# The shift and scale products of an adaLN front: eight weight units asked for at once, multiplied unsplit in four parts of the array

## The chip, the cores and the metric

The kernel runs on one core of one Trainium2 chip. The metric is device time in microseconds (us) of one execution. Before the change it was 1428.91 us, the median of three runs (1427.53 to 1434.31).

## The reference

One layer of a diffusion trunk over 256 latent and 256 context tokens of width 1024. What the change touches is the first step, the modulation vectors, and the projection that needs two of them:

```python
silu_c = jax.nn.silu(c)
silu_cc = jax.nn.silu(c_ctx)
sh1_l, sc1_l, g1_l, sh2_l, sc2_l, g2_l = jnp.split((silu_c @ w_ada[l] + b_ada[l])[:, None, :], 6, axis=-1)
sh1_c, sc1_c, ... = jnp.split((silu_cc @ w_ada[l] + b_ada[l])[None, None, :], 6, axis=-1)
pl = (xl * (1.0 + sc1_l) + sh1_l) @ w_in[l]
pc = (xc * (1.0 + sc1_c) + sh1_c) @ w_in[l]
yc, yl = token_mixers(pc, pl, ...)        # Hyena, short convolution, GLA, gated DeltaNet
xl = layer_norm(DN_ALPHA * xl + g1_l * (yl @ w_out[l]), ...)
fl = moe_ffn(xl * (1.0 + sc2_l) + sh2_l, ...)   # top 4 of 32 experts, all 32 are streamed
```

`w_ada` is 1024 x 6144 in fp32. Sections 0 and 1 of its columns (shift and scale, 8 MB) are needed for both vectors, `c` and `c_ctx`, before any projection can start. The other four sections are needed for `c` alone and much later.

## The kernel before

The program has two halves. The front (0 to about 375 us) makes the modulation vectors, the projections and the four token mixers. The expert stage (the rest) streams 384 units of 1 MB of expert weights through a ring of 16 places. The front's work is written as six generators that `weave` advances by a fixed string `ORDER`; what each engine executes, and in which order, is settled when the program is built. All loads go out on one queue, SP's, in program order; SP stops at a load whose place is not free yet.

A weight unit is 128 partitions x 2 rows x 1024 columns (1 MB) and lies in one of four places r0 to r3. `first_ada` names the eight units of sections 0 and 1, `('ada', sec, h)`, and `queues` deals them to the four places, two to a place. `issue(spot)` loads the next unit of a place and whatever `beside` ties to it; `done(key)`, called where a unit has been used for the last time, issues the next one of that place. So the second unit of a place is asked for after the product of the first, and the unit that follows (`uB`, the weights of the first projection B, or `uada` of section 2, the first of the late sections) after the product of the second.

`ada_first` multiplies the units. Of the two k rows of a unit one (`kk` = 0) is split: ACT copies it rounded to fp32r (`hi`, line 434), DVE subtracts to get `lo` (line 435), and TensorE multiplies both with the 4 columns of `s4` (line 438). The other row is multiplied as plain fp32 with the 2 columns of `sT3` (line 429). Both go to rows 0 to 3 of two PSUM banks. `ada_tail` copies these 4 rows out (lines 449 and 451), turns them with eight transposes (line 455) and adds bias and halves (lines 458 to 461). The result is `mod`.

Then `prep` modulates the inputs `xu` chunk by chunk (`modulate`, lines 543 to 545: ACT makes hi, DVE lo), splits the weights (`split`, lines 552 and 553: `hlB`), and `proj_toks` multiplies (lines 557 to 559, `pB`), 12 products of 432 columns for each of 8 chunks k. In between, ACT and POOL work on the late sections: `ada_late` scales a unit on ACT (line 643) and adds it up on POOL (lines 645, 647); its place is then loaded again. These steps stand in ACT's order between chunks of B: the first unit of section 2 after the third chunk.

Of the kernel before, what the change touches and what calls it, by code (L numbers as in the profile page):

```python
# [11 lines left out]
F32 = mybir.dt.float32  # L12
# [11 lines left out]
D = 1024  # L24
# [174 lines left out]
def trunk(ctx: ExitStack, tc: tile.TileContext, I, out, offs, dbg=None, nexp=NE):  # L199
# [65 lines left out]
    def load(dst, src):  # L265
        nc.sync.dma_start(dst, src)
# [17 lines left out]
    load(va[:, 0:64], I['va'][:, 0:64])  # L284

# [23 lines left out]
    beside['ada', 1, 3] = [(xus[0], xT[0])]  # L309
    beside['B', 0] = [(xus[1], xT[1])]  # L310
# [4 lines left out]
    first_ada = [('ada', sec, h) for sec in range(2) for h in range(4)]  # L315
# [7 lines left out]
    def issue(spot):  # L323
# [21 lines left out]
        for dst, src in beside.pop(key, []):  # L345
            load(dst, src)
        open_units[key], spot_of[key] = u, spot

    def take(key):
        return open_units[key]  # L350

    def done(key):

        issue(spot_of[key])

    for spot in range(4):
        issue(spot)

# [47 lines left out]
    sT = cst.tile([128, 16], F32, name="sT")  # L406
# [3 lines left out]
    s4 = cst.tile([128, 8, 4], F32R, name="s4")  # L410
    sT3 = sT.rearrange("p (k v) -> p k v", v=2)
    S_.activation(s4[:, :, 0:2], sT3, AF.Copy)
    V.tensor_sub(s4[:, :, 2:4], sT3, s4[:, :, 0:2])


    def ada_first():

        tails = []
        for sec in range(2):
            ps = [(bank, fbank)[sec](f"psada{sec}{n}") for n in range(2)]  # L420
            for h in range(4):
                if sec == 1:
                    next(tails[0], None)
                u = take(('ada', sec, h))
                for kk in range(2):
                    k = 2 * h + kk
                    if kk:
                        for n in range(2):
                            P_.matmul(ps[n][0:2], sT3[:, k], u[:, kk, n * 512:(n + 1) * 512], start=False, stop=(k == 7), skip_group_check=True)  # L429
                        done(('ada', sec, h))  # L430
                    else:
                        w2 = early([128, 2, D], F32R, (0, 1, 3)[(4 * sec + h) % 3], f"adap{sec}{k}")
                        hi, lo = w2[:, 0], w2[:, 1]
                        S_.activation(hi, u[:, kk], AF.Copy)
                        V.tensor_sub(lo, u[:, kk], hi)
                        for w in (hi, lo):
                            for n in range(2):
                                P_.matmul(ps[n][0:4], s4[:, k], w[:, n * 512:(n + 1) * 512], start=(k == 0 and w is hi), stop=False, skip_group_check=True)  # L438
                    yield
            tails.append(ada_tail(sec, ps))  # L440
        yield from tails.pop()
        have.add('mod')

    def ada_tail(sec, ps):

        r4 = fp.tile([128, D], F32, tag="kTn", name=f"r4{sec}")[0:4]
        for n in range(2):
            if sec and n:
                V.tensor_copy(r4[:, n * 512:(n + 1) * 512], ps[n][0:4])
            else:  # L450
                S_.activation(r4[:, n * 512:(n + 1) * 512], ps[n][0:4], AF.Copy)
        yield
        pt = xbank(f"psadT{sec}")
        for c in range(8):
            P_.transpose(pt[:, 4 * c:4 * c + 4], r4[:, c * 128:(c + 1) * 128], ident[0:4, 0:4])
        yield
        p4 = pt[:, 0:32].rearrange("p (c v) -> p c v", v=4)
        V.tensor_tensor(mod[:, sec], p4[:, :, 0:2], bada[:, 8 * sec:8 * sec + 8].unsqueeze(2).to_broadcast([128, 8, 2]), op=OP.add)
        V.tensor_tensor(mod[:, sec], mod[:, sec], p4[:, :, 2:4], op=OP.add)
# [241 lines left out]
    mst = early(list(I["masks"].shape), I32, 3, "mst")  # L701
    load(mst, I['masks'])
# [1407 lines left out]
```

## Time and profile before

| | us |
|---|---|
| median of 3 runs | 1428.91 |
| lowest, highest | 1427.53, 1434.31 |
| the profiled execution | 1435.11 |
| its span in the profile | 1433.3 |
| TensorE busy (81% of the span) | 1156.2 |
| ACT busy | 298.1 |
| DVE busy | 485.9 |

The profile is one execution; its span is the time from the first to the last recorded instruction, 1.8 us short of that execution's own time. TensorE's busy share is an average over two halves that have little in common, so it is not a limit by itself. What matters for the change stands in the first 60 us, of which the page's 40 slices (36 us each) show only two digits; these have to be read from the timeline and from narrower stretches. The moved bytes of a stretch are its GB/s times its length.

### The profile page before, as it was taken

The page shows a single profiled execution, that of the slowest core. Times are in us where ns is not written, and L with a number is a line of the kernel's source. Part 1 is how long each engine was busy: PE and PEld are TensorE (multiplying, and loading weights), DVE is VectorE, ACT ScalarE, POOL GpSimd, SP SyncE. Part 2 cuts the span into 40 slices and gives each one's busy share as a digit, 9 for nine tenths or more (in the row PEclk, how much of TensorE's full clock was granted, in tenths as well). Part 3 has the DMA queues.
Part 4 walks back from the last instruction along what each step waited for, and adds up shares of the span by engine and source line. Part 5 has one row for each costly group of instructions (what it writes and reads, how often), then busy time and mean ns, then how long its engine had stood idle before and what let it go on. Part 6 is the DMA issues. An engine that isn't in the chain of part 4 may idle for free.

```text
span 1433.3 us, 26137 instructions
## 1 busy us (share of the span) xinstructions
PE 1156.2 (81%) x11226; PEld 713.9 (50%) x11226; DVE 485.9 (34%) x857; ACT 298.1 (21%) x576; POOL 191.0 (13%) x233
## 2 busy tenths in 40 slices
PE   5797999889687897878698988777676979777883
PEld 0576888678544544445344633344333544444442
DVE  3767667978521211211020221121121111211116
ACT  2556644444210110101010111010001101001112
POOL 0242233440200100001000100000000100000002
PEclk9998879999698998989699999897869989877896
DMA  7733334427796998999965999999999999999960
GB/s 275 254 110 123 119 119 149 149 95 293 307 418 264 410 419 352 419 416 418 378 235 192 417 419 418 417 416 419 418 413 418 406 411 420 399 418 419 417 264 29
DMA packets 129056, 460.56 MB, mean 321 GB/s; under 512 B 9488, under 2 KB 19088, under 8 KB 128048
## 3 DMA queue, kind: packets, MB, share of 16 engines
q1 hardware_dynamic: 128816, 457.52, 80.4%
q8 instruction: 131, 2.15, 0.6%
q14 instruction: 109, 0.89, 0.2%
HBM read 456.45 MB, written 1.05 MB: 319 GB/s over the span
## 4 chain that ended last, share of the span: by engine, by line
PE 53%; DMA 24%; DVE 11%; issue 8%; ACT 4%; SPq 0%; DVEq 0%; ACTq 0%
PE g L1768 17%; DMA ring<-in_w_down 12%; PE four L1768 12%; DMA ring<-in_w_up 8%; PE xb L1750 6%; PE four L1814 2%; DMA ring<-in_w_gate 2%; PE fb L1786 2%; PE psada L429 1%; DMA bd<-in_b_down 1%; DMA uada<-in_w_ada 1%; PE psW L1005 1%; DVE gt L1794 1%; ACT scr L1796 1%; PE psada L438 1%
## 5 line engine op out<-in xcount | busy, mean ns | idle before, releaser
L1768 PE MATMUL g<-ring,X 128*32 128x256 f32 (+1 forms) x3680 | 350.1, 466 | 141.7 <-issue 89.0
L1768 PEld LDWEIGHTS g<-ring,X 128*32 128x32 f32 (+1 forms) x3680 | 153.8, 127 | 319.6 <-issue 228.6
L1768 PE MATMUL four<-ring,X 128*32 128x256 f32 (+1 forms) x2272 | 211.1, 440 | 20.0 <-DMA ring<-in_w_down 19.0
L1824 DVE SCALAR_TENSOR_TENSOR rows<-four,cw,rows 128x1024 f32<-128x1024 f32 x62 | 76.7, 1279 | 339.9 <-PE four L1814 339.9
L1794 DVE TENSOR_TENSOR gt<-fb,vc 128x256 f32<-128x256 f32 (+1 forms) x37 | 18.6, 504 | 405.1 <-PE fb L1786 405.1
L1750 PEld LDWEIGHTS xb<-Sg,hl 128*128 128x128 f32 x1024 | 133.8, 211 | 29.2 <-issue 26.5
L1768 PEld LDWEIGHTS four<-ring,X 128*32 128x32 f32 (+1 forms) x2272 | 86.3, 119 | 123.7 <-issue 61.5
L1750 PE MATMUL xb<-Sg,hl 128*128 128x96 f32 x1024 | 143.9, 300 | 4.7 <-DVE Sg L1736 2.6
L1736 POOL TENSOR_SCALAR Sq<-slots,rank 128x128 f32<-128x128 f32 x62 | 39.5, 648 | 563.4 <-PE xb L1758 333.5
L1772 ACT ACTIVATE sA<-g 128x256 f32<-128x256 f32 (+1 forms) x33 | 14.0, 423 | 331.3 <-PE g L1768 331.3
L1736 POOL TENSOR_SCALAR Sg<-slots,rank 128x96 f32<-128x96 f32 x62 | 31.7, 523 | 307.3 <-PE xb L1750 271.0
L645 POOL TENSOR_TENSOR adas<-adas,uada 128x1024 f32<-128x1024 f32 x24 | 59.1, 2464 | 100.7 <-ACT uada L643 100.3
L1752 ACT ACTIVATE X<-xb 128x384 f32<-128x384 f32 x64 | 31.4, 491 | 132.6 <-PE xb L1750 127.1
L1796 ACT ACTIVATE scr<-gt 128x256 f32<-128x256 f32 (+1 forms) x37 | 17.7, 480 | 158.7 <-DVE gt L1795 158.7
L1814 PE MATMUL four<-sA,ST 32*128 32x256 f32 (+1 forms) x512 | 46.5, 440 | 1.8 <-DVE sA L1988 1.8
L1772 ACT ACTIVATE sA<-four 128x256 f32<-128x256 f32 (+1 forms) x30 | 12.8, 427 | 167.3 <-PE four L1768 167.3
L643 ACT ACTIVATE uada<-uada,sT 128x1024 f32<-128x1024 f32 x32 | 35.7, 1142 | 9.8 <-DMA uada<-in_w_ada 9.8
L1005 PEld LDWEIGHTS <-before 64*64 64x64 f16 x1088 | 29.9, 116 | 9.8 <-issue 4.0
L1814 PEld LDWEIGHTS four<-sA,ST 32*128 32x128 f32 (+1 forms) x512 | 30.1, 206 | 7.6 <-DVE sA L1988 2.3
L1802 DVE TENSOR_TENSOR X<-fb,vc 128x256 f32<-128x256 f32 (+1 forms) x36 | 18.0, 499 | 41.3 <-PE fb L1786 41.3
L1797 DVE TENSOR_TENSOR gt<-gt,scr 128x256 f32<-128x256 f32 (+1 forms) x37 | 18.9, 510 | 21.9 <-ACT scr L1796 21.9
L1786 PE MATMUL fb<-cons,sB 128*128 128x128 f32 x76 | 15.5, 300 | 7.4 <-ACT sB L1772 7.4
(565 smaller groups left out, 1558.7 us busy)
## 6 DMA issues: line engine op xcount, KB each, us to landing
ring<-in_w_gate SPq DMA_DIRECT2D x128, 1024.0 KB, 18.0
ring<-in_w_up SPq DMA_DIRECT2D x128, 1024.0 KB, 17.8
ring<-in_w_down SPq DMA_DIRECT2D x128, 1024.0 KB, 18.3
uada<-in_w_ada SPq DMA_DIRECT2D x24, 1024.0 KB, 5.4
uout<-in_w_out SPq DMA_DIRECT2D x4, 1024.0 KB, 4.8
uE<-in_w_in SPq DMA_DIRECT2D x2, 1024.0 KB, 5.5
uF<-in_w_in SPq DMA_DIRECT2D x4, 512.0 KB, 4.0
uG<-in_w_in SPq DMA_DIRECT2D x2, 1024.0 KB, 5.2
```

Source lines behind the costliest of these rows:

```text
L643: S_.activation(u[:, kk], u[:, kk], AF.Copy, scale=sT3[:, 2 * h + kk, 0:1])
L645: G_.tensor_tensor(acc_, acc_, u[:, kk], op=OP.add)
L1005: P_.matmul(ps[cs, x * 64:x * 64 + 64], L[cs, x], R[cs, x] if len(R.shape) == 3 else R[cs], start=True, stop=True, skip_group_check=True)
L1736: eng.tensor_scalar(Sm[:, t, 0:m * n].rearrange("p (q s) -> p q s", s=n), slots[:, a:a + n].unsqueeze(1).to_broadcast([128, m, n]), rank[: ...
L1750: P_.matmul(xb[:, o:o + n], hl[:, t, k * 128:(k + 1) * 128], Sm[:, t, 0:n], start=(k == ks[0] and t == 0), stop=(t == 1), skip_group_check ...
L1752: S_.activation(X[:, ks[0] * n:(ks[-1] + 1) * n], xb[:, 0:len(ks) * n], AF.Copy)
L1768: P_.matmul(ps[n * q:n * q + n, 0:m], x(k), w[:, kk * 1024 + q * m:kk * 1024 + (q + 1) * m], start=(k == 0), stop=(k == 7), skip_group_che ...
L1786: P_.transpose(fb[:, c * 128:(c + 1) * 128], s[:, c * 128:(c + 1) * 128], ident)
L1794: V.tensor_tensor(g, p, bias(Cv('bg'), e, n), op=OP.add)
L1796: S_.activation(sg, g, AF.Sigmoid, scale=1.702)
L1814: P_.matmul(four[:, b, t * 256:(t + 1) * 256], st_[n * q:n * q + n, t * 128:(t + 1) * 128], Y[n * q:n * q + n, i * 256:(i + 1) * 256], sta ...
L1824: V.scalar_tensor_tensor(a, ps[t], cw[:, t, e:e + 1], a, op0=OP.mult, op1=OP.add)
```

## The change

All eight units of sections 0 and 1 are asked for at the start. The four of section 1 get places of their own for this: three ring places that are used later (r4, r5, r7) and a half of the buffer `pa`. The input `xT` (two loads) and the masks follow at once, the masks in the buffer `pb` instead of a ring place. `queues` then holds, behind the first unit of each place, what stood behind the second.

The product is no longer split. `s32` is a stationary operand of 32 columns, of which 2 are used and 30 are zero. The four products of a unit (2 rows x 2 halves of 512 columns) go to four 32-row parts of one PSUM bank, and so to four 32-column parts of the array, as plain fp32. Where a unit took 6 products before (4 of hi and lo, one record each in the profile, and 2 plain ones, two records each), it now takes 4 plain ones: 8 records before and after, of 512 columns each. The tail copies the whole bank (128 x 512) on ACT, turns it with four 128 x 128 transposes and adds the two parts that belong together, and the bias, on DVE.

The tile `s4` (128 bytes a partition) goes and `sT` grows by 128, so that what is allocated behind them starts where it did: all ring places stay 256 bytes above a multiple of 512. Which of the eight ring places lies where is permuted, since a place is laid out when it is first named.

```diff
+    extra = [early([128, 2048], F32, i, f"uada1{i}") for i in (0, 1, 3)] + [pa[:, 2048:4096]]
...
-    beside['ada', 1, 3] = [(xus[0], xT[0])]
-    beside['B', 0] = [(xus[1], xT[1])]
...
-    first_ada = [('ada', sec, h) for sec in range(2) for h in range(4)]
+    first_ada = [('ada', 0, h) for h in range(4)]
...
+        if key[0:2] == ('ada', 0):
+            h = key[2]
+            open_units['ada', 1, h], spot_of['ada', 1, h] = extra[h].rearrange("p (k f) -> p k f", k=2), None
...
     for spot in range(4):
         issue(spot)
+    for h in range(4):
+        load(take(('ada', 1, h)), w_ada[:, 2 * h:2 * h + 2, D:2 * D])
+    mst = pb[:, 2048:2048 + I["masks"].shape[1]].bitcast(I32)
+    for dst, src in ((xus[0], xT[0]), (xus[1], xT[1]), (mst, I['masks'])):
+        load(dst, src)
...
-    sT = cst.tile([128, 16], F32, name="sT")
+    sT = cst.tile([128, 48], F32, name="sT")[:, 0:16]
...
-    s4 = cst.tile([128, 8, 4], F32R, name="s4")
-    S_.activation(s4[:, :, 0:2], sT3, AF.Copy)
-    V.tensor_sub(s4[:, :, 2:4], sT3, s4[:, :, 0:2])
+    s32 = pb[:, 3200:3456].rearrange("p (k v) -> p k v", v=32)
+    V.memset(s32, 0.0)
+    V.tensor_copy(s32[:, :, 0:2], sT3)
...
-                    k = 2 * h + kk
-                    if kk:
-                        for n in range(2):
-                            P_.matmul(ps[n][0:2], sT3[:, k], u[:, kk, n * 512:(n + 1) * 512], start=False, stop=(k == 7), skip_group_check=True)
-                        done(('ada', sec, h))
-                    else:
-                        w2 = early([128, 2, D], F32R, (0, 1, 3)[(4 * sec + h) % 3], f"adap{sec}{k}")
-                        hi, lo = w2[:, 0], w2[:, 1]
-                        S_.activation(hi, u[:, kk], AF.Copy)
-                        V.tensor_sub(lo, u[:, kk], hi)
-                        for w in (hi, lo):
-                            for n in range(2):
-                                P_.matmul(ps[n][0:4], s4[:, k], w[:, n * 512:(n + 1) * 512], start=(k == 0 and w is hi), stop=False, skip_group_check=True)
-                    yield
+                    for n in range(2):
+                        q = 2 * kk + n
+                        P_.matmul(ps[32 * q:32 * q + 32], s32[:, 2 * h + kk], u[:, kk, n * 512:(n + 1) * 512], start=(h == 0), stop=(h == 3), skip_group_check=True)
+                done(('ada', sec, h))
+                yield
...
-        r4 = fp.tile([128, D], F32, tag="kTn", name=f"r4{sec}")[0:4]
...
+        r = t512(f"r{sec}")
+        S_.activation(r, ps, AF.Copy)
...
-        for c in range(8):
-            P_.transpose(pt[:, 4 * c:4 * c + 4], r4[:, c * 128:(c + 1) * 128], ident[0:4, 0:4])
+        for c in range(4):
+            P_.transpose(pt[:, 128 * c:128 * c + 128], r[:, c * 128:(c + 1) * 128], ident)
```

SP's order, before, from the last load of the first batch (`mst`, the masks) to the first projection's second unit. `uada_1_h` is unit h of section 1, `xu0` and `before0` the two halves of the input, `uB_0` and `uB_1` the units of B; in brackets the semaphores that a load waits for, of which DMAHW0 to DMAHW7 count the completion of earlier loads:

```order
L266 DMA mst_119<-in_masks 128x1152
L266 DMA uada_1_0_150<-in_w_ada 128x2x1024 [waits DMAHW0_49,DMAHW1_49,DVE_49,PE_49]
L266 DMA uada_1_1_185<-in_w_ada 128x2x1024 [waits DMAHW3_49,DVE_49,PE_49]
L266 DMA uada_1_2_196<-in_w_ada 128x2x1024 [waits DMAHW2_49,DMAHW4_49,DVE_49,PE_49]
L266 DMA uada_1_3_207<-in_w_ada 128x2x1024 [waits DMAHW5_49,DVE_49,PE_49]
L266 DMA xu0_92<-in_xT 128x2048
L266 DMA uB_0_224<-in_w_in 128x4x384 [waits DMAHW0_49,DVE_49,PE_49]
L266 DMA uB_0_224<-in_w_in 128x4x32 [waits DMAHW6_49]
L266 DMA uB_0_224<-in_w_in 128x4x16 [waits DMAHW7_49]
L266 DMA before0_84<-in_xT 128x2048
```

The same stretch now, from the first unit of section 1 (`uada10`; `uada11`, `uada13` and `before0<-in_w_ada` are the other three):

```order
L266 DMA uada10_87<-in_w_ada 128x2x1024
L266 DMA uada11_88<-in_w_ada 128x2x1024 [waits DMAHW0_49]
L266 DMA uada13_89<-in_w_ada 128x2x1024 [waits DMAHW1_49]
L266 DMA before0_84<-in_w_ada 128x2x1024 [waits DMAHW2_49]
L266 DMA xu0_95<-in_xT 128x2048 [waits DMAHW3_49]
L266 DMA before0_84<-in_xT 128x2048 [waits DMAHW4_49]
L266 DMA before1_85<-in_masks 128x1152 [waits DMAHW5_49]
L266 DMA uB_0_151<-in_w_in 128x4x384 [waits DMAHW6_49,PE_49]
L266 DMA uB_0_151<-in_w_in 128x4x32 [waits DMAHW7_49]
L266 DMA uB_0_151<-in_w_in 128x4x16 [waits DMAHW0_49]
```

The four units of section 1, the input and the masks no longer wait for PE or DVE, only each for the load that stands eight before it. The loads behind them (`uB_1`, `vb`, `cons`, then `uada_2_0`, the first unit of section 2) stand in the same order in both programs.

TensorE's order, before, from the last split row to the first product of B (`psada` are the products of section 1, `psadT1` its transposes, `pB0` the first bank of B):

```order
L438 MATMUL psada10_210<-adap16_274,s4_110 4x512 [waits Activation_49]
L438 MATMUL psada11_211<-adap16_274,s4_110 4x512
L438 MATMUL psada10_210<-adap16_274,s4_110 4x512 [waits DVE_49]
L438 MATMUL psada11_211<-adap16_274,s4_110 4x512
L429 MATMUL psada10_210<-uada_1_3_207,sT_106 2x512 [waits DMAHW3_49]
L429 MATMUL psada11_211<-uada_1_3_207,sT_106 2x512
L455 MATMUL psadT1_286<-cons2_89,r41_283 128x4 [waits Activation_49]
L455 MATMUL psadT1_286<-cons2_89,r41_283 128x4 x3
L455 MATMUL psadT1_286<-cons2_89,r41_283 128x4 [waits DVE_49]
L455 MATMUL psadT1_286<-cons2_89,r41_283 128x4 x3
L557 MATMUL pB0_298<-hlB0_308,xl0_115 128x432 [waits Activation_49]
```

The same place now, from the last but one unit:

```order
L438 MATMUL psada1_199<-uada13_89,before1_85 32x512 [waits DMAHW1_49]
L438 MATMUL psada1_199<-uada13_89,before1_85 32x512 x3
L438 MATMUL psada1_199<-before0_84,before1_85 32x512 [waits DMAHW2_49]
L438 MATMUL psada1_199<-before0_84,before1_85 32x512 x3
L452 MATMUL psadT1_235<-cons2_92,r1_233 128x128 [waits DVE_49,Activation_49]
L452 MATMUL psadT1_235<-cons2_92,r1_233 128x128 x3
L556 MATMUL pB0_243<-hlB0_253,xl0_124 128x432 [waits Activation_49]
```

A unit's product now waits for the unit's load alone; before, it waited for ACT and DVE too. Behind the first product of B the orders of all engines are the same as before.

## Rows read from the trace of the kernel before

**Rows 1.** The chain of waits from 44 to 56 us (start, us, what).

```profile
43.80 1.82 PE psada L429 x4
45.64 8.20 DMA uada<-in_w_ada
```

**Rows 2.** The timeline of SP (start, us, what it issues).

```profile
4.82 0.46 SPq L266 DMA_DIRECT2D mst<-in_masks  x1
15.02 16.63 SPq L266 DMA_DIRECT2D uada<-in_w_ada  x4
...
45.64 13.37 SPq L266 DMA_DIRECT2D uada<-in_w_ada  x2
```

**Rows 3.** Stretches of the first 54 us: busy times, granted clock, DMA share, GB/s.

```profile
core 0: us, PE busy (x) PEld busy (x) DVE busy (x) ACT busy (x) POOL busy (x), PEclk, DMA share, GB/s
0.00:53.80 53.80, 36.06 (x99) 9.74 (x100) 24.17 (x48) 16.71 (x25) 1.40 (x5) 0.90 0.81 293
0.00:6.00 6.00, 0.00 (x0) 0.00 (x0) 0.36 (x2) 1.72 (x3) 0.19 (x4) 1.00 0.64 192
6.00:16.00 10.00, 7.59 (x14) 1.11 (x14) 4.58 (x8) 2.53 (x3) 0.00 (x0) 1.00 1.02 418
20.00:26.00 6.00, 5.32 (x9) 0.85 (x10) 2.54 (x3) 2.31 (x3) 0.00 (x0) 0.51 0.00 0
28.00:36.00 8.00, 5.73 (x17) 0.95 (x16) 2.36 (x2) 4.09 (x5) 0.00 (x0) 1.00 1.01 357
36.00:52.00 16.00, 12.70 (x49) 4.61 (x48) 9.72 (x24) 6.07 (x11) 0.00 (x0) 0.93 1.00 356
52.00:54.00 2.00, 2.00 (x9) 1.89 (x8) 1.93 (x6) 0.14 (x1) 0.00 (x0) 0.70 0.16 66
```

**Rows 4.** The timeline of ACT around the first chunks of B.

```profile
47.45 0.60 ACT L543 ACTIVATE xl<-xu,mod 128x256 fp32r<-128x256 f32 x1 [2.07 <-DMA vb<-in_vb]
...
51.33 0.55 ACT L552 ACTIVATE hlB<-uB 128x432 fp32r<-128x432 f32 x1
53.86 2.19 ACT L643 ACTIVATE uada<-uada,sT 128x1024 f32<-128x1024 f32 x2 [1.99 <-DMA uada<-in_w_ada]
...
64.28 2.18 ACT L643 ACTIVATE uada<-uada,sT 128x1024 f32<-128x1024 f32 x2
```

**Rows 5.** Groups by line and shape, 0 to 48 us (busy us, mean ns | idle before).

```profile
L429 PE MATMUL psada<-uada,sT 128*2 128x512 f32 x32 | 18.4, 705 | 0.0
L438 PE MATMUL psada<-adap,s 128*4 128x512 f32 x32 | 10.4, 442 | 10.7 <-ACT adap L434 9.8 <-DVE adap L435 0.9
L434 ACT ACTIVATE adap<-uada 128x1024 fp32r<-128x1024 f32 x8 | 8.2, 1049 | 8.8 <-DMA uada<-in_w_ada 8.8
L451 ACT ACTIVATE r<-psada 4x512 f32<-4x512 f32 x3 | 1.8, 587 | 15.0 <-PE psada L429 15.0
```

**Rows 6.** The timeline, single rows of TensorE and DVE.

```profile
21.72 3.57 PE L429 MATMUL psada<-uada,sT 128*2 128x512 f32 x4
...
49.05 0.46 PE L557 MATMUL pB<-hlB,xl 128*128 128x432 f32 x1 [2.26 <-ACT hlB L552]
...
56.58 2.17 DVE L544 TENSOR_SCALAR xu<-xu,mod 128x256 f32<-128x256 f32 x1 [2.14 <-ACT xl L543]
...
395.53 1.07 PE L1768 MATMUL g<-ring,X 128*32 128x256 f32 x16
```

**Rows 7.** Transposes of 128 x 128, by line (ns min/median/max).

```profile
L1011 PE MATMUL pstk<-cons,kvT x8: 270/272/276, 111.2 to 112.7; 128*128 128x128 f32 x8
```

**Rows 8.** TensorE alone in stretches of B (busy, granted clock, DMA share, GB/s).

```profile
50.00:53.00 3.00, 2.68 (x7) 0.50 0.67 268
53.00:70.00 17.00, 13.51 (x66) 0.99 0.54 187
70.00:77.00 7.00, 5.92 (x16) 0.52 0.78 257
```

**Rows 9.** One stretch of the expert stage, columns as in rows 3.

```profile
1000.00:1100.00 100.00, 79.53 (x612) 39.37 (x602) 16.21 (x27) 9.51 (x21) 6.43 (x12) 0.83 1.03 417
```

More of the change, by code (lines that the diff above doesn't have):

```diff
@@ L352, in done @@
     def done(key):
-        issue(spot_of[key])
+        if spot_of[key] is not None:
+            issue(spot_of[key])
     for spot in range(4):
         issue(spot)
+    for h in range(4):
[3 more added lines that the diff above has]
+        load(dst, src)
     places = {}
@@ L419, in ada_first @@
         for sec in range(2):
-            ps = [(bank, fbank)[sec](f"psada{sec}{n}") for n in range(2)]
+            ps = (bank, fbank)[sec](f"psada{sec}")
             for h in range(4):
@@ L424, in ada_first @@
                 u = take(('ada', sec, h))
+                yield
                 for kk in range(2):
-                    k = 2 * h + kk
-                    if kk:
-                        for n in range(2):
-                            P_.matmul(ps[n][0:2], sT3[:, k], u[:, kk, n * 512:(n + 1) * 512], start=False, stop=(k == 7), skip_group_check=True)
-                        done(('ada', sec, h))
-                    else:
-                        w2 = early([128, 2, D], F32R, (0, 1, 3)[(4 * sec + h) % 3], f"adap{sec}{k}")
-                        hi, lo = w2[:, 0], w2[:, 1]
-                        S_.activation(hi, u[:, kk], AF.Copy)
-                        V.tensor_sub(lo, u[:, kk], hi)
-                        for w in (hi, lo):
-                            for n in range(2):
-                                P_.matmul(ps[n][0:4], s4[:, k], w[:, n * 512:(n + 1) * 512], start=(k == 0 and w is hi), stop=False, skip_group_check=True)
-                    yield
+                    for n in range(2):
+                        q = 2 * kk + n
+                        P_.matmul(ps[32 * q:32 * q + 32], s32[:, 2 * h + kk], u[:, kk, n * 512:(n + 1) * 512], start=(h == 0), stop=(h == 3), skip_group_check=True)
+                done(('ada', sec, h))
+                yield
             tails.append(ada_tail(sec, ps))
@@ L444, in ada_tail @@
     def ada_tail(sec, ps):
-        r4 = fp.tile([128, D], F32, tag="kTn", name=f"r4{sec}")[0:4]
[L447 to L451, printed above, removed]
+        r = t512(f"r{sec}")
+        S_.activation(r, ps, AF.Copy)
         yield
         pt = xbank(f"psadT{sec}")
-        for c in range(8):
-            P_.transpose(pt[:, 4 * c:4 * c + 4], r4[:, c * 128:(c + 1) * 128], ident[0:4, 0:4])
+        for c in range(4):
+            P_.transpose(pt[:, 128 * c:128 * c + 128], r[:, c * 128:(c + 1) * 128], ident)
         yield
-        p4 = pt[:, 0:32].rearrange("p (c v) -> p c v", v=4)
-        V.tensor_tensor(mod[:, sec], p4[:, :, 0:2], bada[:, 8 * sec:8 * sec + 8].unsqueeze(2).to_broadcast([128, 8, 2]), op=OP.add)
-        V.tensor_tensor(mod[:, sec], mod[:, sec], p4[:, :, 2:4], op=OP.add)
+        p4 = pt.rearrange("p (c k n v) -> p k n c v", c=4, k=2, n=2)[:, :, :, :, 0:2]
+        m = mod[:, sec].rearrange("p (n c) v -> p n c v", n=2)
+        b = bada[:, 8 * sec:8 * sec + 8].rearrange("p (n c) -> p n c", n=2).unsqueeze(3).to_broadcast([128, 2, 4, 2])
+        V.tensor_tensor(m, p4[:, 0], b, op=OP.add)
+        V.tensor_tensor(m, m, p4[:, 1], op=OP.add)
         if sec == 1:
@@ L698, in rsqrt2 @@
         V.scalar_tensor_tensor(dst, u, 3.0, less, op0=OP.subtract, op1=OP.mult)
-    mst = early(list(I["masks"].shape), I32, 3, "mst")
-    load(mst, I['masks'])
     G_.tensor_copy(masks, mst)
```

## The prediction

> **What bounds the kernel now.** I read the stretches first, then SP's timeline, then the chain and ACT's timeline around 50 us. Through the first 54 us everything goes over one stream of loads, and that stream stops. It moves 418 GB/s from 6 to 16 us and nothing from 20 to 26 [rows 3], because SP put nothing more into the queue: the first batch was out at 4.82 + 0.46 us, the next unit was asked for at 15.02, and the four units of section 1 took until 31.7 to be asked for, each after a product on TensorE [rows 2]. The page's DMA digits for the first slice (7 tenths) hide this hole.
>
> The chain between 44 and 56 us shows what the delay costs: the last product of the shift and scale ends at 45.62, and what follows is the load of the first unit of section 2, 8.20 us [rows 1]. ACT stands still for it 1.99 us, until 53.86, with the fourth chunk of B queued behind it [rows 4]; DVE waits 2.14 us for that chunk in turn and then works on B without a pause [rows 6]. So the place to watch is not the moment at which `mod` is ready, 47.45 at the latest [rows 4], but the landing of that unit. What comes later (the mixers, then the expert stage, which streams at 417 GB/s, a DMA share of 1.03 [rows 9]) keeps its order and is moved as a whole. Where it starts earlier, it ends earlier.
>
> **The loads.** Until that unit has landed, both programs load the same bytes: 293 GB/s over 53.8 us [rows 3] are 15.76 MB. In both it is the last of them. Its last bytes come at about 52.4 us (66 GB/s for the last 2 us are 0.13 MB, 0.4 us at 356 GB/s [rows 3]), and ACT starts 1.5 us behind that.
>
> Now no load before B waits for TensorE. The order shows that a load waits for the one eight places ahead of it; with seven or eight asked for, mostly of 1 MB, the stream does not run dry. So the first 16 us stay as they are: 192 x 6 + 418 x 10 give 5.33 MB [rows 3], and 10.43 MB remain. From there the rate decides, and the trace has two. With a batch of eight out it was 418; from 28 to 36 and from 36 to 52, with few loads out and B's small ones among them, 357 and 356, at a DMA share of 1.00 all the same [rows 3].
> - All at 418: 10.43 / 0.418 = 25.0, the unit lands at 16 + 25.0 + 1.5 = 42.5.
> - All at 356: 29.3, it lands at 46.8.
> - By kind: up to the masks 6.60 MB at 418 (15.8 us, to 31.8), then B's two units, vb, cons and the unit itself, 3.83 MB by their shapes, at 356 (10.8 us): 42.6 + 1.5 = 44.1.
>
> I take 44.6, the middle of the two ends, which lies next to the value by kind. Against 53.86 ACT's step is 9.2 us earlier; the ends give 7.1 and 11.4.
>
> The Trainium skill has a rule that speaks for the low end ("DMA: Bandwidth & Descriptors", section "Where 436 GB/s comes from"): the fabric could carry about 435 GB/s, but from HBM a core gets about 358. The trace does not bear it out as a limit, since 418 and 417 stand in rows 3 and 9. By it the unit would land at 46.6 and the gain would be 7.2, inside the ends above.
>
> **The products.** ACT loses eight copies of 1049 ns (8.2 us), DVE their eight differences, TensorE 18.4 + 10.4 us of products [rows 5]. None of that is a term of the sum, since the loads now set the pace. What is added on TensorE is 8 records of 512 columns for each unit, in four parts. Nearest row: in the expert stage 16 records of 256 columns, four parts as well, the same number of columns, take 1.07 us [rows 6]. That is at full clock; at half it is 2.1, still less than the 2.5 us in which 1.05 MB come at 418. The other end is no overlap at all: four plain records of 512 columns took 3.57 us at half clock [rows 6], so 7.1 a unit. I take 1.07 to 2.1, the row with the four parts.
>
> The last unit of section 1 is the ninth MB: 9.24 MB by 16 + 3.91 / 0.418 = 25.4, landed at 26.9. Behind it: product 1.1 to 2.1, the copy on ACT (587 ns for the same 512 columns [rows 5]; 128 partitions instead of 4, taken as the same), four transposes of at most 272 ns each, twice that at half clock [rows 7], three small DVE steps, and hand-overs of some 0.2 us: 3 to 6 us. `mod` is ready between 30 and 33. B's first unit lands at 31.8 + 0.885 / 0.356 + 1.5 = 35.8. So the products and the longer tail are hidden by 3 to 6 us; from there on each us more would move the first chunk, and from some 7 us on the fourth as well, because ACT needs only 4.4 us for three chunks (47.45 to 51.88 [rows 4]).
>
> B's first product moves from 49.05 [rows 6] to about 36.4, 12.6 us. Of that lead 3.4 us are given back at once: ACT is through with three chunks at about 39.3 and then waits some 5.3 us for the unit of section 2 instead of 1.99. What is late next is therefore the same load as before, and the gain is that of the load, 9.2. The next unit is asked for when POOL has used the first, moves with it, and was in time before (ACT took it at 64.28 without a wait [rows 4]).
>
> **Rest.** The masks are turned by POOL some 16 us later; POOL has nothing else until the unit of section 2. Clearing `s32` falls before the first unit has landed. The changed `sT` keeps all that is allocated behind it in place, and the permuted ring places differ by multiples of 8 KB. I find nothing in the rows that would tell one place from another: 0, with no bound but the two of the loads.
>
> **Sum.** Profiled execution 1435.11, span 1433.3; less 9.2 gives 1425.9. It lies 6.2 above the median of the runs; I take the same difference from the median: 1428.91 - 9.2 = 1419.7.
>
> **Rivals.**
> 1. B's start decides, not the unit (gain 12.6, 1416.3). For it: TensorE then has three chunks behind it early, and ACT's wait could be made up where ACT was ahead before. Against it: DVE follows ACT chunk by chunk and showed no slack after 56.58 [rows 6]. 0.10.
> 2. TensorE stays at half clock in B. The granted clock was 0.50 to 0.52 from 50 to 53 and from 70 to 77 us, both times after TensorE had stood still, and 0.99 in between, under steady work [rows 8]. Now TensorE has short products with gaps until 27 us, nothing until 36, and a second gap before the fourth chunk. A record of B takes 0.38 us at half clock (2.68 / 7) and 0.20 at full (13.51 / 66). In the first three chunks 36 records at half are 13.7 us, to 50.1, about when DVE has the fourth chunk ready (56.58 + 2.17 less 9.2, and some 1.7 more, 51.2): hidden. In the other five, 60 records more at half cost up to 10.8, of which the kernel before paid about 3.4 already (7 us at 0.52). The gain falls to between 2 and 6; 1424.9 in the middle. Against it: under steady work the clock came back. The Trainium skill says the same of gaps between bursts ("TensorE: Matmul & The Clock Gate", section "HAM oscillation — how this bites in real kernels"): each burst then begins at the low clock. Rows 8 agree. By it alone the first chunks of B are slow, which is hidden. 0.20.
> 3. The stream does not keep even 356, since B's small loads (rows of 64 and 128 bytes) queue behind each other's completion. At 330 for all that remains: 31.6 us, lands at 49.1, gain 4.8, 1424.1. Against it: 357 was held with three loads out [rows 3]. 0.10.
> 4. Slower: the four parts do not overlap, and the clock stays low. Then a unit costs 7.1 us, eight 57, from 6 us on; with a tail of 6 `mod` is ready at 69 instead of 47.45, and the end moves by 21.6 less the 1.99 that ACT waits now: 1428.9 + 19.6 = 1448.5. It decides from 4.7 us a unit on ((49.4 - 12) / 8). Against it: 1.07 [rows 6]. 0.05.
>
> **How the numbers follow.** The forecast has 0.55, its own range 1417.5 to 1421.8. A difference of 0.5% (7.1 us) is about what a measurement of this kernel can tell from no change, given runs from 1427.5 to 1434.3. Faster: forecast and rival 1, 0.65, less 0.01 for a median that falls badly; same: rivals 2 and 3 and that 0.01, 0.31; rival 4 is 0.05 slower with little in between, and I give slower 0.05. The range for 8 in 10 runs from 1414.5 (rival 1, and the scatter of a median) to 1426.0 (the weaker half of rival 2 stays out).
>
> **What would show it.** Right: no stretch without bytes before 42 us; a rate near 418 to 31 us; the products of a unit within 2.2 us, each ended by its load; ACT's scaling of the first unit of section 2 at 42.5 to 46.8, after a wait of 3 us or more; the expert stage's first load some 9 us earlier. Wrong: a hole in the stream, `mod` later than 36 us, B at half clock beyond its third chunk, or a front that ends 9 us earlier and an end that does not.

## The result, and the profile after

The changed kernel takes 1414.52 us (median of 4 runs, 1413.83 to 1415.62) against 1428.22 us for the kernel before on the same chip; the ratio is 0.9906, with a 95% interval from 0.9878 to 0.9934. That is 13.7 us, where 9.2 were forecast. In a second timing on another chip it was 1417.11 against 1428.13 us, 0.9922 [0.9893, 0.9952], 11.0 us. Both intervals lie below 1: the change makes the kernel faster, by 1.8 to 4.5 us more than the term that I had worked out.

First the stretches of the changed kernel, in the columns of [rows 3]:

```profile
0.00:53.80 53.80, 28.30 (x124) 15.25 (x125) 20.89 (x54) 15.84 (x29) 3.74 (x6) 0.85 0.83 313
6.00:16.00 10.00, 4.08 (x12) 0.77 (x12) 4.45 (x12) 0.55 (x2) 0.00 (x0) 1.00 1.02 415
20.00:26.00 6.00, 5.02 (x44) 1.23 (x36) 2.48 (x8) 0.60 (x1) 0.00 (x0) 1.00 1.03 424
28.00:36.00 8.00, 0.66 (x4) 0.42 (x4) 2.11 (x7) 1.73 (x5) 1.14 (x1) 0.68 1.05 384
36.00:52.00 16.00, 12.01 (x41) 10.09 (x42) 9.48 (x19) 10.62 (x21) 2.41 (x1) 0.71 0.52 174
```

The stretch from 20 to 26 us, in which nothing moved, now has 424 GB/s. The other thing to see is the granted clock, the third number from the end: 0.68 and 0.71 from 28 to 52 us, which was 0.93 to 1.00 before. SP (start, us, what it issues) shows why the stream holds:

```profile
4.84 4.53 SPq L266 DMA_DIRECT2D uada<-in_w_ada  x3
9.41 2.29 SPq L266 DMA_DIRECT2D before<-in_w_ada  x1
...
16.53 18.04 SPq L266 DMA_DIRECT2D uB<-in_w_in  x6
...
35.69 13.74 SPq L266 DMA_DIRECT2D uada<-in_w_ada  x2
```

Section 1 is asked for by 11.7 us instead of 31.7 [rows 2]. TensorE's and ACT's timelines answer to [rows 6] and [rows 4]:

```profile
26.43 1.06 PE L438 MATMUL psada<-before,before 128*32 128x512 f32 x8 [1.42 <-DMA before<-in_w_ada]
...
36.13 0.73 PE L556 MATMUL pB<-hlB,xl 128*128 128x432 f32 x1 [7.26 <-ACT hlB L551]
...
63.57 0.46 PE L558 MATMUL pB<-hlB,xl 128*128 128x432 f32 x1 [1.25 <-DVE hlB L552]
```

```profile
29.53 0.60 ACT L542 ACTIVATE xl<-xu,mod 128x256 fp32r<-128x256 f32 x1 [1.37 <-DVE mod L460]
...
38.41 0.55 ACT L551 ACTIVATE hlB<-uB 128x432 fp32r<-128x432 f32 x1
44.34 2.19 ACT L642 ACTIVATE uada<-uada,sT 128x1024 f32<-128x1024 f32 x2 [5.38 <-DMA uada<-in_w_ada]
...
56.40 2.18 ACT L642 ACTIVATE uada<-uada,sT 128x1024 f32<-128x1024 f32 x2
...
66.68 1.28 ACT L1137 ACT_TABLE_LOAD   x1
```

The unit of section 2 is taken at 44.34 us instead of 53.86, 9.5 us sooner, behind a wait of 5.38 us. ACT's table load (`ACT_TABLE_LOAD`) that follows the end of B is the mark of B's end in what follows: it stands at 66.68; before it stood at 79.28 (row below). That is 12.6 us. (The other profiled execution of the changed kernel has 43.98 and 66.37.) So the load's 9.5 us became 12.6 by the end of B, and that difference is what had to be explained. These are the rows of the kernel before that show the end of B, first of TensorE, then of ACT:

```profile
71.08 0.73 PE L559 MATMUL pB<-hlB,xl 128*128 128x432 f32 x1 [3.21 <-DVE hlB L553]
```

```profile
79.28 1.28 ACT L1140 ACT_TABLE_LOAD   x1
```

Before, TensorE stood still for 3.21 us and then went through most of the last two chunks at 0.52 [rows 8]. After, the stop of 1.25 us at 62.3 is followed by full clock:

```profile
50.00:53.00 3.00, 2.43 (x7) 0.50 0.93 280
53.00:66.00 13.00, 11.76 (x58) 0.93 0.65 225
66.00:77.00 11.00, 10.42 (x73) 1.00 0.40 138
```

Each stop stands behind two operations of DVE that take 2.50 to 2.74 us instead of 0.4 to 0.6 while POOL adds up the second unit. First the kernel before, where they belong to the last chunk but one, then the changed one, where they belong to the last:

```profile
65.84 2.52 DVE L545 TENSOR_TENSOR xc<-before,xc 128x256 fp32r<-128x256 f32 x1
68.28 2.74 DVE L553 TENSOR_TENSOR hlB<-uB,hlB 128x432 fp32r<-128x432 f32 x1
```

```profile
57.90 2.50 DVE L543 TENSOR_SCALAR before<-before,mod 128x256 f32<-128x256 f32 x1
60.44 2.56 DVE L544 TENSOR_TENSOR xc<-before,xc 128x256 fp32r<-128x256 f32 x1
```

### The profile page after: what moved, and what is told of

Same layout as the page of the kernel before. It is cut to its first block, busy times and chain, and to the rows that moved or that the text cites. A ratio compares the mean times of both kernels' runs of the same rounds, so it can differ in the third digit from the quotient of the medians.

```text
span 1413.8 us, 26088 instructions
## 1 busy us (share of the span) xinstructions
PE 1119.7 (79%) x11218; PEld 696.0 (49%) x11218; DVE 473.7 (34%) x849; ACT 288.9 (20%) x566; POOL 191.8 (14%) x233
## 4 chain that ended last, share of the span: by engine, by line
PE 49%; DMA 28%; DVE 10%; issue 8%; ACT 4%; SPq 1%; DVEq 0%; ACTq 0%
PE g L1765 17%; DMA ring<-in_w_down 13%; PE four L1765 11%; DMA ring<-in_w_up 8%; PE xb L1747 5%; DMA ring<-in_w_gate 3%; PE four L1811 2%; PE fb L1783 2%; DMA before<-in_w_ada 1%; DMA bd<-in_b_down 1%; DMA uada<-in_w_ada 1%; SPq L266 1%; PE psW L1002 1%; DVE hlo L552 1%; DVE gt L1791 1%
## 5 line engine op out<-in xcount | busy, mean ns | idle before, releaser
L1765 PE MATMUL g<-ring,X 128*32 128x256 f32 (+1 forms) x3680 | 357.1, 470 | 155.5 <-issue 95.9
L1765 PE MATMUL four<-ring,X 128*32 128x256 f32 (+1 forms) x2272 | 201.6, 421 | 16.8 <-DMA ring<-in_w_down 15.6
L1747 PEld LDWEIGHTS xb<-Sg,hl 128*128 128x128 f32 x1024 | 123.7, 198 | 27.1 <-issue 24.3
L1747 PE MATMUL xb<-Sg,hl 128*128 128x96 f32 x1024 | 133.2, 285 | 4.3 <-DVE Sg L1733 2.6
L1811 PE MATMUL four<-sA,ST 32*128 32x256 f32 (+1 forms) x512 | 42.7, 407 | 4.0 <-DVE sA L1985 4.0
```

What stands on the lines that cost most here:

```text
L1747: P_.matmul(xb[:, o:o + n], hl[:, t, k * 128:(k + 1) * 128], Sm[:, t, 0:n], start=(k == ks[0] and t == 0), stop=(t == 1), skip_group_check ...
L1765: P_.matmul(ps[n * q:n * q + n, 0:m], x(k), w[:, kk * 1024 + q * m:kk * 1024 + (q + 1) * m], start=(k == 0), stop=(k == 7), skip_group_che ...
L1811: P_.matmul(four[:, b, t * 256:(t + 1) * 256], st_[n * q:n * q + n, t * 128:(t + 1) * 128], Y[n * q:n * q + n, i * 256:(i + 1) * 256], sta ...
```

## The experiments

The first question was whether the loads alone make the gain, as I had forecast, or whether the lighter product has a part in it. For what the load does not explain there was the clock theory: the half clock at the end of B, which the kernel before pays, is gone.

**The two halves apart.** The first kernel has the requests of the changed one and the split product of before; the second has the unsplit product and the requests of before.

```
e1:  load(take(('ada', 1, h)), ...) ahead of B, as in the change
     ada_first() with hi, lo copies and products of 4 columns, as before
e2:  ada_first() with s32 and four parts of the array, as in the change
     beside[...] and section 1 in the places of section 0, as before
```

> The changed order of loads (eight units asked for at once, input and masks behind them) with the split product and tail of the kernel before; the split halves lie in the buffers that later hold the split weights, two copies of 512 columns instead of one of 1024. Theory A (the stream is what counts): no hole in the stream, the first unit of section 2 lands at 44 to 45 us as in the changed kernel; TensorE needs 2.9 us a unit at full clock and about 5 at half (8 records), so mod comes at 33 to 45 us, and up to 40 this is hidden: 1414 to 1420 us. Theory B (the lighter product is what counts): mod comes no earlier than 45 us, at most a third of the gain is left, 1424 to 1428 us.

> The unsplit product in four parts and its tail, with the requests of the kernel before (each unit of section 1 asked for after a product, the masks in their ring place). Theory A: the hole in the stream stays in part, since units are still asked for one by one; the first product ends at about 11 us instead of 15, the others at 18 to 21, so the hole shrinks from 7 us to 1 to 3 and the first unit of section 2 lands at 46 to 49 us: 1417 to 1423 us. Theory B: the whole gain is there, 1413 to 1416 us. If loads alone and product alone each give most of the gain, then each closes the hole by itself, and their gains do not add up.

Measured on one chip: the loads alone 1422.45 us, ratio 0.9965 [0.9946, 0.9985], 5.0 us by that ratio (3.9 between the medians); the product alone 1418.15 us, 0.9938 [0.9911, 0.9965], 8.8 us (8.2). The loads alone fall between the ranges that were expected; the product alone lies in that of theory A. By the time, the product alone cannot be told from the whole change, since the intervals overlap; the trace shows that neither half makes the whole. ACT with the loads alone:

```profile
45.09 0.60 ACT L548 ACTIVATE xl<-xu,mod 128x256 fp32r<-128x256 f32 x1 [2.08 <-DVE mod L466]
...
49.41 2.18 ACT L648 ACTIVATE uada<-uada,sT 128x1024 f32<-128x1024 f32 x2
```

and with the product alone:

```profile
34.99 0.60 ACT L534 ACTIVATE xl<-xu,mod 128x256 fp32r<-128x256 f32 x1 [1.83 <-DVE mod L452]
...
47.03 2.19 ACT L634 ACTIVATE uada<-uada,sT 128x1024 f32<-128x1024 f32 x2 [7.61 <-DMA uada<-in_w_ada]
```

With the loads alone the unit is there and ACT does not wait for it: `mod` is ready only at 45 us, and the first three chunks stand ahead of the unit. (This kernel makes its split copies in pieces of 512 columns instead of 1024, so its product is not quite the old one.) With the product alone the hole closes nearly by itself, because a place comes free as soon as its short product is done (the four requests of section 1 go out from 11.03 to 22.0 us, in the kernel before from 15.02 to 31.7):

```profile
20.00:26.00 6.00, 4.10 (x32) 0.95 (x24) 2.48 (x8) 0.60 (x1) 0.00 (x0) 1.00 0.93 303
```

So either half is held back by what the other removes: of the 9.5 us at the unit the loads alone give 4.5, the product alone 6.8. The two overlap a little, since their sum is more than the whole. At the end of B the product alone has its table load at 69.40 us, 2.7 behind the changed kernel, as at the unit.

**The clock at the end of B.** The kernel before, with products on constants ahead of chunk 6's `lo` product, first seven, then three:

```
  P_.matmul(d[:, 0:n], xl[:, k, ts], hi[:, 0:n], ...)
+ for _ in range(7):   # 3 in the second kernel; k == 6, t == 0 only
+     P_.matmul(ps, C('ones'), cons2[:, 0:512], start=True, stop=True)
  P_.matmul(d[:, 0:n], xh[:, k, ts], lo[:, 0:n], ...)
```

> The kernel before, with seven extra 128x512 products on TensorE (results unused) placed in the stall of 3.2 us ahead of the seventh chunk of B (67.9 to 71.1 us). Theory C (the shift grew from 9.5 to 12.6 us within B because the kernel before runs its last two chunks at half clock after that stall, and the changed one does not): the granted clock stays near 1.0 from 70 to 77 us, the last product of B ends 3 us earlier, 1425 to 1426 us. Rival (the shift grew for another reason, such as where POOL and DVE meet): clock up, but the next step on ACT and DVE starts when it did, 1428 to 1429 us.

> The kernel before, with three additional 128x512 products on TensorE (on constants, into an accumulator that nobody reads) ahead of chunk 6's last kind of product in B. In the run with seven of them they took 6.17 us (0.88 us each) and ran from 67.94 to 73.55 us, past the 71.08 us at which the operand was ready, so that B ended no sooner although the clock was kept; three take 2.64 us and fit into the 3.21 us stall of TensorE. Clock theory (the half clock of 70 to 77 us stretches the last two chunks of B, and that it is gone after the change is the part of the gain that the load does not explain): granted clock 1.00 in 70 to 77 us, B ends and the table load of ScalarE stands at about 76.4 us instead of 79.3, time 2.5 to 3 us under the kernel before on the same chip, ratio about 0.998. Rival (what ends B is VectorE beside GpSimd's additions, whatever the clock): the table load stays at 79 us, time within 0.5 us of the kernel before.

Seven were a mis-sized experiment: they kept the clock (1.00 from 70 to 77 us) but ran past the moment at which the operand was there, so what they won they also cost. Time 1429.08 us, 1.0013 [0.9993, 1.0034].

```profile
67.94 6.17 PE L624 MATMUL busy<-cons 128*128 128x512 f32 x14
73.55 0.76 PE L637 MATMUL pB<-hlB,xl 128*128 128x432 f32 x1
```

Three fit into the stop. TensorE, then the clock from 70 to 77 us, then ACT:

```profile
66.00 2.74 PE L624 MATMUL busy<-cons 128*128 128x512 f32 x6
69.37 0.47 PE L637 MATMUL pB<-hlB,xl 128*128 128x432 f32 x1 [0.64 <-DVE hlB L553]
```

```profile
70.00:77.00 7.00, 7.00 (x46) 1.00 0.86 296
```

```profile
52.17 2.19 ACT L654 ACTIVATE uada<-uada,sT 128x1024 f32<-128x1024 f32 x2 [1.87 <-DMA uada<-in_w_ada]
...
74.85 1.28 ACT L1151 ACT_TABLE_LOAD   x1
```

The load happened to land 1.7 us sooner in this execution, so the measure is the stretch from the unit to the table load: 25.42 us before (79.28 - 53.86), 22.68 here, 22.34 in the changed kernel. Of the 3.1 us between these executions the clock accounts for 2.7. The time does not resolve it: 1428.7 us, ratio 0.9996 [0.9973, 1.0019], an interval of 3.3 us either way, with 2.7 us (0.9981) inside and the rival's 0 too.

The half clock behind such a stop is also not the same in every execution. Three other traces have a stop at the same place, with the same 22 products behind it: the loads alone, and the two executions of the kernel with another order of requests (below), whose clock from 54 to 60 us was 1.00 in one and 0.72 in the other:

```profile
66.86 0.46 PE L564 MATMUL pB<-hlB,xl 128*128 128x432 f32 x1 [3.19 <-DVE hlB L558]
```

```profile
54.00:60.00 6.00, 4.54 (x23) 4.37 (x24) 3.76 (x8) 1.59 (x3) 0.60 (x1) 1.00 0.72 218
54.00:60.00 6.00, 4.58 (x16) 4.25 (x17) 3.69 (x9) 0.47 (x1) 0.24 (x1) 0.72 0.74 225
```

From the end of the stop to the table load it takes 8.20 us in the kernel before, 7.00 with the loads alone, 5.47 and 7.03 in those two, and 5.48 with the three products. So the half clock cost 2.7 us in the one execution of the kernel before that was profiled, 1.5 in two others and nothing in a fourth, behind stops of 2.88 to 3.41 us. With products in the stop the clock stayed up in both kernels that had them. How much of the change's gain it is on average is not shown.

**The clock at the start of B.** The changed kernel with such products ahead of B's chunks 0 (fourteen) and 3 (nine).

```
+ BUSY = {0: 14, 3: 9}
+ if name == 'B' and k in BUSY: keep_busy(BUSY[k])
```

> The changed kernel with 14 extra products of 128x512 (results unused) ahead of B's first chunk, where TensorE idles from 28.9 to 36.1 us, and 9 ahead of its fourth (45.7 to 48 us). Theory C: the clock stays at full, chunks 4 to 7 run at 0.20 instead of 0.36 us a record, ACT's wait of 2.8 us for TensorE at 52.1 to 54.9 shrinks to under 1, the second unit of section 2 is scaled 2 us earlier, and the end comes 1 to 3 us earlier than in the changed kernel: 1411.5 to 1413.5 us. Rival (DVE and ACT pace B, the clock is hidden): 1414 to 1415 us.

1415.77 us, 0.9926 [0.9897, 0.9956]: no gain over the changed kernel, though the clock was 1.00 from 26 to 77 us, and outside both ranges that were expected. The 23 products again outran the gaps (20.1 us in all), and the table load came at 68.19 instead of 66.68, so this run decides nothing about the clock. Better-sized runs follow below.

**The places.** The scratch tile ahead of the ring at its old size, which puts the ring's places 128 bytes above multiples of 512.

```
- sT = cst.tile([128, 48], F32, name="sT")[:, 0:16]
+ sT = cst.tile([128, 16], F32, name="sT")
```

> The changed kernel with the places of the weight ring 128 bytes above multiples of 512 instead of 256 (the scratch tile ahead of them is 128 bytes smaller). Theory of the prediction (the places are no term of the sum): the rate of 1000 to 1100 us is 417 GB/s as before and the time is that of the changed kernel within 1 us. Rival (the distance to a multiple of 512 matters for the expert stage's stream of 384 MB, some 1000 us): a loss of 0.2% of the stream is 2 us, shown after 380 us only, with the first stages unchanged.

> The changed kernel once more, beside the others on one chip. Same as in its first timing: 13 to 14 us under the kernel before (ratio 0.9905).

The rival holds, and with nine times its price: 1435.4 us, 1.0052 [1.0035, 1.007], 18.3 us above the changed kernel on the same chip (1417.11). Up to 380 us the two do not differ beyond the scatter: the table load behind the front stands at 382.92 us, in the two executions of the changed kernel at 381.43 and 384.73. The page's list of DMA issues, first of this kernel, then of the changed one (the last number is us from issue to landing), and one stretch of the expert stage of this kernel, beside 412 and 415 GB/s in the two executions of the changed one and 417 in [rows 9]:

```profile
ring<-in_w_gate SPq DMA_DIRECT2D x128, 1024.0 KB, 18.6
```

```profile
ring<-in_w_gate SPq DMA_DIRECT2D x128, 1024.0 KB, 18.0
```

```profile
1000.00:1100.00 100.00, 75.45 (x584) 35.22 (x578) 16.21 (x27) 9.11 (x20) 6.59 (x12) 0.85 1.03 404
```

A load takes 3.3% longer at a full DMA share. (The edit moves all that is allocated behind the tile, not the ring alone; the loss shows in the ring's loads.) The Trainium skill has a rule that fits ("DMA: Bandwidth & Descriptors", section "How a descriptor splits into AXI transactions"): a descriptor that does not start on a multiple of 256 bytes pays for the bytes below its start. An estimate from that page for 4 KB at 128 bytes off is 132 beats instead of 128, 3.1%. The page says it of the address that is read, though; what moved here is the place that is written, so that its rule is the cause is argued and not shown. No run here tried a multiple of 512.

**Another order of the requests.** ACT still waits 5.38 us for the unit of section 2. This kernel asks for it behind the first half of B's weights, and for the masks last; POOL converts them behind its first addition.

```
- for dst, src in (..., (xus[1], xT[1]), (mst, I['masks'])):
+ for dst, src in (..., (xus[1], xT[1])):
+ beside['B', 1].append((mst, I['masks']))
...
- done(('ada', sec, h))
+ if (sec, h) != (0, 1): done(('ada', sec, h))
+ if (sec, h) == (0, 2): done(('ada', 0, 1))
...
+ if (sec, h) == (2, 0): G_.tensor_copy(masks, mst)
...
- G_.tensor_copy(masks, mst)
```

> The changed kernel with another order of requests only: the first half of B's weights, then the first unit of section 2, then the second half of B's weights and the small ones; the masks are asked for last and converted behind the first addition of GpSimd. Theory (the first unit of section 2 still ends B's longest wait, since ScalarE stands 5.38 us for it at 38.96 to 44.34 us): the unit lands at about 37 us instead of 44.3, ScalarE takes it at 38.9 us without a wait, B ends 4 to 5 us sooner (table load at about 62 us instead of 66.7), time 4 to 5 us under the changed kernel: 1409.5 to 1410.5 us. Rival (the clock and VectorE's pace beside GpSimd bound B by now, and the second half of B's weights comes too late): ScalarE waits for the second half of B's weights instead, B ends within 2 us of 66 us, time 1412.5 us or more.

> The changed kernel with the first unit of section 2 asked for behind the first half of B's weights, once more, beside the next three on one chip: 4 to 5 us under the changed kernel, so 15 to 18 us under the kernel before (ratio 0.988 to 0.989).

1412.4 us against 1417.11 for the changed kernel on that chip, 0.9887 [0.986, 0.9914]: 4.7 us less, as the theory expected. On another chip it was 1411.87 us, 0.9904 [0.9886, 0.9922], short of the 0.988 to 0.989 that were expected there and no better than the first timing of the changed kernel (0.9906). So the theory holds in the trace: the unit is taken without a wait, and the table load stands at 60.93 and 62.45 us in the two executions, against 66.68 and 66.37. How much of that arrives in the time is not settled. ACT, DVE, POOL and TensorE of the first execution:

```profile
37.49 2.17 ACT L646 ACTIVATE uada<-uada,sT 128x1024 f32<-128x1024 f32 x2
...
60.93 1.28 ACT L1142 ACT_TABLE_LOAD   x1
```

```profile
40.19 2.15 DVE L547 TENSOR_SCALAR xu<-xu,mod 128x256 f32<-128x256 f32 x1 [0.66 <-ACT xl L546]
...
49.82 2.53 DVE L547 TENSOR_SCALAR before<-before,mod 128x256 f32<-128x256 f32 x1
52.38 2.51 DVE L548 TENSOR_TENSOR xc<-before,xc 128x256 fp32r<-128x256 f32 x1
```

```profile
39.74 2.45 POOL L650 TENSOR_TENSOR adas<-uada 128x1024 f32<-128x1024 f32 x1 [39.31 <-ACT uada L646]
```

```profile
55.46 0.46 PE L562 MATMUL pB<-hlB,xl 128*128 128x432 f32 x1 [3.41 <-DVE hlB L556]
```

What is late next is DVE: three of its operations take 2.15 to 2.53 us, where such a one takes 0.41 to 0.43, each while POOL adds up the scaled units.

**Three kernels on top of it.** One keeps TensorE busy ahead of B with seven products, one puts POOL's first three additions on DVE, one does both.

```
e7: + if name == 'B' and k == 0: keep_busy(7)
e8: - G_.tensor_tensor(acc_, ...)
    + (V if sec == 2 and h < 2 else G_).tensor_tensor(acc_, ...)
```

> The kernel of e6 with seven additional 128x512 products on TensorE (6.2 us, from 28.6 to 34.8 us) between the last product of the modulation and the first of B. Clock theory: TensorE keeps 1.00 over 26 to 42 us (0.87 and 0.65 in e6). What it gives back is only what ScalarE waits for accumulators in chunks 4 to 6 of e6 (0.15 + 0.80 + 0.49 = 1.4 us): B ends 1.4 us sooner (table load at 59.5 us instead of 60.9), 1411 us against e6's 1412.4. Rival (VectorE paces chunks 0 to 7, so that the clock there costs nothing): clock 1.00, table load within 0.5 us of 60.9 us.

> The kernel of e6 with the additions of the first two units of section 2 (three of 128x1024) on VectorE instead of GpSimd. In e6 an operation of VectorE beside GpSimd's additions takes 2.15, 2.53 and 2.51 us instead of 0.41 to 0.43, and TensorE then waits 3.41 us for hlB. Theory (the two engines stand in each other's way, and VectorE alone does both in less time: 128x512 takes 0.68 us there, so 128x1024 some 1.3 us): no operation of B on VectorE above 0.7 us, wait of TensorE about 1.2 us, B ends 2.2 us sooner (table load at 58.7 us instead of 60.9), time 2 us under e6: 1410. Rival (three additions of 1.3 us on VectorE in order cost what the stretch cost, and VectorE waits for ScalarE's scaling besides): table load at 61 us or later, time that of e6 or above.

> The kernel of e6 with both: the seven products that keep TensorE busy and the three additions on VectorE. If both theories hold: table load at 57.3 us, 1409 us, 3.5 us under e6. If only one does, that one's gain; if neither, e6's 1412.4 us.

With TensorE kept busy: 1413.26 us, 0.9913 [0.9897, 0.993], nothing gained over 1411.87. The clock was 1.00 from 26 to 42 us (0.87 and 0.65 without), and the table load stood at 61.78 us, between the 60.93 and 62.45 of the kernel under it. Those two lie further apart than the 1.4 us that were looked for. Nor did the clock stay up: behind a stop of 1.80 us for DVE it fell between 42 and 50 us, and ACT then waited 3.30 us for TensorE. So this run alone does not decide.

```profile
42.00:50.00 8.00, 5.85 (x22) 4.89 (x21) 7.79 (x15) 4.70 (x11) 2.21 (x2) 0.79 0.74 241
```


With the additions on DVE: 1407.44 us, 0.9863 [0.9845, 0.988], 4.4 us under 1411.87, and the two intervals do not meet. DVE, TensorE and ACT:

```profile
39.68 1.22 DVE L651 TENSOR_TENSOR adas<-uada 128x1024 f32<-128x1024 f32 x1 [0.17 <-ACT uada L646]
...
51.69 2.55 DVE L649 TENSOR_TENSOR adas<-adas,uada 128x1024 f32<-128x1024 f32 x2
```

```profile
54.81 0.46 PE L562 MATMUL pB<-hlB,xl 128*128 128x432 f32 x1 [0.42 <-DVE hlB L556]
```

```profile
57.92 1.28 ACT L1143 ACT_TABLE_LOAD   x1
```

DVE does the additions itself in 3.8 us (1.22 + 2.55); beside POOL it lost 5.9 (7.19 for three operations that take 0.43 each). The stop of TensorE shrinks from 3.41 to 0.42 us, and B ends 3.0 us sooner than in the first execution of the kernel under it (4.5 than in the second), where 2.2 were expected. One operation of DVE still took 1.30 us, beside POOL's conversion of the masks. Both together give 1407.77 us, 0.9879 [0.986, 0.9898], no more than the additions alone, although the clock was 1.00 from 26 to 60 us; from the unit to the table load it took 20.59 us, with the additions alone 20.44, at a clock of 0.70 from 26 to 36 and 0.64 from 36 to 42. There the rival holds: half clock at the start of B costs nothing, because TensorE is not what is late. The kernel with the additions on DVE has the lowest ratio of all. Its interval ends at 0.988, where that of the changed kernel's first timing begins (0.9878); from the kernel with both it cannot be told.

## Why the prediction was right, and where a step failed

**The place to watch: right.** The unit of section 2 landed and was taken at 44.34 us, forecast 44.6; ACT waited 5.38 us, forecast 5.3. The stream had no hole, 418 GB/s from 6 to 32 us, then 362 to 36 us and 375 to 42; that the stream goes slower with B's small loads in it was seen rightly. Of the eight units' products the first took 1.93 us, the next four 5.20 together, the last three 0.96 to 1.06 each, inside the 1.07 to 2.1 that were taken or a little below. `mod` was used from 29.53 and B began at 36.13 (forecast 30 to 33, and 36.4). Rivals 3 and 4 did not come. Rival 1's time, 1416.3, is nearer to the 1414.5 than the forecast's 1419.7, but not by its mechanism: B's start moved by 12.9 us, and 3.4 of it were given back at the unit, as forecast.

**The size of the gain: partly luck.** The term of the sum was 9.2 us and measured 9.5 at the unit, but the gain was 13.7 us, in the second timing 11.0. Both times lie below the forecast's own 1417.5 to 1421.8, and 1414.52 falls on the lower end of the wide range, 1414.5. That end was set for rival 1 and the scatter of a median, not for what came.

**The signs.** Most came: no stretch without bytes, a rate near 418 to 31 us, the products within 2.2 us, the unit at 44.34 behind a wait of more than 3 us. The expert stage's first load was asked for 15.7 and 12.3 us earlier in the two executions, not some 9. That each product is ended by its load was so for the last unit alone; four of them stood in TensorE's order behind a product of another chain until 17.38 us. And one sign of being wrong came: B was at half clock beyond its third chunk, 0.50 from 50 to 53 us.

**"None of that is a term of the sum": half wrong.** It holds only beside the other half of the change. With the split product kept, `mod` is the place to watch after all, 45.09 us, and the loads alone give 5.0 of the 11 to 13.7 us. The forecast used the short product for its `mod` at 30 to 33 and then credited the loads alone with the result. The number was not hurt, the reason was.

**"Keeps its order and is moved as a whole": this failed.** The shift grew from 9.5 us at the unit to 12.6 at the end of B. The text had the size of it in hand: in rival 2 it put the half clock from 70 to 77 us at 3.4 us that the kernel before pays already. It counted the clock only as a danger and never as something that could go away. In the profiled executions it went, because DVE's stretched operations now fall onto the last chunk and stop TensorE for 1.25 us instead of 3.21, and full clock followed; three products in that stop give the kernel before 2.7 of the 3.1 us. The loss that rival 2 feared, half clock in the first chunks and in the fourth, did come (0.50 to 0.71). It even moved the stop: ACT waited 2.81 us for TensorE in B instead of 1.16, so the second unit was scaled 12.06 us behind the first instead of 10.42, POOL's additions came as much later, and DVE was a chunk further by then. That this is why the stop is shorter is read from these rows; no run tested it. With another order of the requests and the additions on DVE, keeping the clock up at the start of B gained nothing, as that rival's first half said.

**The rest at 0: right, but what it hangs on was not seen.** The text says that `sT` keeps all in place, and found nothing that tells one place from another. Places 128 bytes above multiples of 512 instead of 256 cost 18 us, which turns the gain into a loss.

**What stays open.** From 12.6 us at the end of B the shift goes to 13.6 at 100 us in one profiled execution of the changed kernel and stays at 12.9 in the other. All of these are against the one profiled execution of the kernel before, which paid the half clock at the end of B in full; others may pay less. The medians, 13.7 and 11.0 us, lie on both sides, and no run was made to settle it.

## What to carry to other kernels

A stop of a few microseconds on TensorE can cost twice if work is queued behind it, once for the wait and once for the half clock that may follow (2.7, 1.5 or 0 us here). When a change moves such a stop, price the clock in both directions, and check in the trace whether TensorE is what is late there: only then is it worth anything. When a change takes tiles out, see where those behind them now begin.

## What was not expected of the hardware

DVE beside POOL's additions of 128x1024 (2.4 to 2.6 us each) does not slow down in proportion but waits: an operation of 0.41 us took 2.12 to 2.56. In the kernel with another order of requests the one that began at 40.19 ended at 42.34 us, 0.15 behind the end of POOL's addition (39.74 + 2.45). The Trainium skill says the same ("SBUF — State Buffer", section "SBUF: two separate sides"): the two share a pair of ports, and the loser blocks for the whole instruction. The run with the additions on DVE agrees, 3.0 us at the end of B.

Part of the scatter of the runs has a place. In some profiled executions TensorE is at half clock for 10 us in the mixers, in others at full, with the same instructions there; five of the fourteen stood at 0.50 to 0.58 there, both of the changed kernel and that of the fastest among them, one at 0.73, eight at 1.00. First the kernel before, then that kernel with the seven products, at the same place of the program:

```profile
183.00:193.00 10.00, 10.00 (x57) 9.28 (x57) 4.41 (x7) 2.52 (x5) 2.36 (x1) 0.50 0.48 159
```

```profile
183.00:193.00 10.00, 9.64 (x162) 8.60 (x161) 6.86 (x12) 6.08 (x10) 2.38 (x1) 1.00 0.48 158
```

The scaling of a late unit on ACT that stands at 182.38 us in the first is 0.2 us earlier in the second; the one at 210.50 is 6.8 us earlier. So the start of a late stage is no measure of a change of 5 us; a landmark close to the edit is.
